# Layer with retention and windowed attention: conditioning sums gathered on VectorE, gate weights loaded later, a new order of the first microseconds, and the first block's mixed rows on VectorE

## The chip, the cores and the metric

The kernel runs on one core of a Trainium2 chip. The metric is device time in microseconds (us) of one execution. The engines are TensorE (PE, with its weight loads shown apart as PEld), VectorE (DVE), ScalarE (ACT), GpSimd (POOL) and SyncE (SP, which here only issues transfers). Each executes its own queue of instructions in order and waits there for data and buffers of the others.

## The reference, cut to what matters

One layer works on 2048 latent tokens of 1024 features and 256 context tokens. It is modulated by a conditioning vector `c`, or `c_ctx` for the context.

```python
shift, scale, gate = split(silu(c) @ w_ada + b_ada, 3)         # 1024 each
shift_c, scale_c, gate_c = split(silu(c_ctx) @ w_ada + b_ada, 3)
h  = rms_norm(x)   * (1 + scale)   + shift                     # 2048 x 1024
hc = rms_norm(ctx) * (1 + scale_c) + shift_c                   # 256 x 1024
rq, rk, rv, rg, aq, ak, av, ag = project(h, w_in)              # 1024 -> 3328 columns
_, crk, crv, _, _, cak, cav, _ = project(hc, w_in)
rq, rk, aq, ak = axial_rope(rq), axial_rope(rk), axial_rope(aq), axial_rope(ak)
s_fwd, s_bwd = retention_final_state(crk, crv, ...)            # starting states
ret_x = retention_branch(rq, rk, rv, rg, s_fwd, s_bwd)         # both directions, group norm, SiLU gate
att_x = windowed_gqa(aq, ak, av, cak, cav, sink) * silu(ag)    # window of 128 beside all context keys
x = x + gate * (concat(ret_x, att_x) @ w_out)
return rms_norm(x) * final_norm_w
```

## The kernel before, in words

Every matrix product is in three passes of TensorE: each fp32 operand is held as a rounded high part and a low part (the operand minus its high part), and the passes are high by high, high by low and low by high (`PASSES`). So each projection weight costs a rounding and a subtraction of 128x512 pieces, four of each for one weight of 1024x256. `load_w` does that: `hi` says who rounds, `lo` who subtracts, and with `lo="mix"` GpSimd takes the second piece of each of the two loads. `split` does the same to a projected, rotated tile (`hi_aq`, `lo_aq`).

The 2048 tokens are four groups of 512 (3, 2, 1, 0; group 3 first). The kernel has these stages.

**Start.** The tokens of group 3 come in transposed (`h2x`, eight feature slices `k` of 128x512), and so do the small parameters (`pr`) and the row of `c` (`row`). The sum of squares over features (`ss_x`) is made by four matmuls with ones on the pairwise sums of squares, and the diagonal blocks are taken out by VectorE (`own_x`). `roots` turns it into 1/rms (a power on GpSimd, `r_x`) and four diagonal tiles (`dg_x`), and `spread` puts the roots on all partitions (`rr_x`). Matmuls on ones (`warm`) fill TensorE's time meanwhile. `silu_row` spreads the row over the partitions (`pc`, then SiLU into `row`). For each `k`, `ada` loads two 128x1024 pieces of `w_ada` (`wss`) and `weigh` makes of each, with the row, one column of 128 sums: shift and scale of that slice (`mod`). `modulate` then makes the high and low parts of `h` (`h3h`, `h3l`), and TensorE puts them through the first three weights (`rg0`, `rq0`, `rq1`, the tiles `frg`, `frq`), whose pieces come in as `wr_s` and are split on the way.

**Projections of groups 3 and 2, with the context beside them.** TensorE goes through the weights `aq1`, `rq0`, `rq1`, then the context's `crk` and `crv` and the groups' `rk` and `rv`, for each of two pairs of heads. Beside that runs a list `spare` of small jobs, of which `background()` takes one after each unit: the context's norm, then eight jobs `column(k)`, each with two `weigh` of 128x1024 by `c_ctx` (`wss`, `room` holds the row), the modulation of one slice and its split into `hc`, and then nine jobs of `gate_columns`: the row of `c` once more and eight `weigh` for the gate (`wgt`, sums in `gcol`). In this stage every second `weigh` is done by GpSimd as a product, with the sum taken by a pass of ScalarE.

**Projections of groups 1 and 0**, and then **sixteen blocks of 128 tokens**: scores `S` of window and context keys, softmax, transposes, values, retention, and the output projection `pz`. The attention scores of the first blocks are woven into the last gate projection by the strings of `WEAVE`: one character pair per unit, `04s` standing for pieces of work put at step k=0. For the first block (b=0) of retention `first` holds keys, queries and states, and `ret_out` makes the gated retention rows `gr` and splits them into `mr` (high and low), from which `pz` starts.

## Time and profile before

| what | value |
|---|---|
| median of the three runs shown | 1163.0 us (1161.56 to 1398.94) |
| the profiled execution: time | 1162.4 us |
| the profiled execution: span in the trace | 1160.6 us |
| PE, DVE, ACT, POOL busy | 97%, 68%, 40%, 34% of the span |
| mean granted TensorE clock | 0.99 of full speed |

All stretches and starts below are us from the start of the span. The profiled execution has 1.8 us outside its span, and lies 0.6 us under the median.

### The profile page before, as it was taken

The page shows a single profiled execution, that of the slowest core. Times are in us where ns is not written, and L with a number is a line of the kernel's source. Part 1 is how long each engine was busy: PE and PEld are TensorE (multiplying, and loading weights), DVE is VectorE, ACT ScalarE, POOL GpSimd, SP SyncE. Part 2 cuts the span into 40 slices and gives each one's busy share as a digit, 9 for nine tenths or more (in the row PEclk, how much of TensorE's full clock was granted, in tenths as well). Part 3 has the DMA queues.
Part 4 walks back from the last instruction along what each step waited for, and adds up shares of the span by engine and source line. Part 5 has one row for each costly group of instructions (what it writes and reads, how often), then busy time and mean ns, then how long its engine had stood idle before and what let it go on. Part 6 is the DMA issues. An engine that isn't in the chain of part 4 may idle for free.

```text
span 1160.6 us, 18086 instructions
## 1 busy us (share of the span) xinstructions
PE 1130.3 (97%) x6290; PEld 974.3 (84%) x6290; DVE 792.4 (68%) x1884; ACT 467.8 (40%) x1026; POOL 399.9 (34%) x517
## 2 busy tenths in 40 slices
...
GB/s 318 322 153 264 234 232 310 168 146 87 158 198 180 182 93 99 151 104 150 88 118 276 69 177 249 106 135 133 136 131 133 133 132 132 132 132 132 96 56 36
DMA packets 139537, 182.24 MB, mean 157 GB/s; under 512 B 11315, under 2 KB 103091, under 8 KB 139318
## 3 DMA queue, kind: packets, MB, share of 16 engines
...
q14 instruction: 42, 0.34, 0.1%
...
## 4 chain that ended last, share of the span: by engine, by line
PE 80%; DVE 9%; DMA 4%; POOL 2%; ACT 2%; issue 2%; SPq 0%; POOLq 0%; DVEq 0%; ACTq 0%
PE pz L1209 14%; PE rv L354 8%; PE rk L341 8%; PE ag L341 6%; PE o L1172 6%; PE pt L1159 5%; PE aq L341 5%; PE rg L341 4%; PE rq L341 4%; PE S L743 3%; PE S L747 2%; PE u L470 2%; PE ak L341 2%; DVE wss L215 2%; PE av L341 1%
## 5 line engine op out<-in xcount | busy, mean ns | idle before, releaser
L765 POOL TENSOR_SCALAR p<-p,m 128x640 f32<-128x640 f32 (+1 forms) x128 | 102.2, 799 | 83.6 <-DVE m L764 82.4
L756 ACT ACTIVATE p<-p,m 128x641 f32<-128x641 f32 (+1 forms) x128 | 104.6, 817 | 62.5 <-DVE m L753 62.1
L1161 ACT ACTIVATE phl<-pt 128x512 fp32r<-128x512 f32 x156 | 92.6, 595 | 79.3 <-PE pt L1159 76.3
L1162 DVE TENSOR_TENSOR phl<-pt,phl 128x512 fp32r<-128x512 f32 x156 | 106.2, 682 | 24.1 <-ACT phl L1161 23.5
L749 DVE CUSTOM_DVE_ANT_0 p<-S,msk 128x640 f32<-128x640 f32 (+1 forms) x128 | 102.4, 800 | 13.1 <-PE S L747 6.9
L1209 PE MATMUL pz<-wg1h,ma 128*128 128x512 f32 x256 | 106.1, 419 | 0.1
L1209 PE MATMUL pz<-wg0h,mr 128*128 128x512 f32 x256 | 103.9, 409 | 1.3 <-POOL mr L109 0.8
L1159 PE MATMUL pt<-ident,p 128*128 128x128 f32 x624 | 93.2, 272 | 0.0
L1159 PEld LDWEIGHTS pt<-ident,p 128*128 128x128 f32 x624 | 75.3, 140 | 8.4
L743 PE MATMUL S<-kwin,aq 128*128 128x384 f32 (+1 forms) x256 | 79.4, 332 | 0.1
L446 ACT ACTIVATE vw<-v,wdec 128x128 fp32r<-128x128 f32 x128 | 43.6, 394 | 80.1 <-DVE v L459 80.1
L747 PE MATMUL S<-kctx,aq 128*128 128x256 f32 x256 | 71.1, 280 | 0.0
L1172 PE MATMUL o<-phl,vwin 128*128 128x512 f32 x184 | 62.2, 416 | 1.3 <-DVE phl L1162 0.8
L1209 PEld LDWEIGHTS pz<-wg0h,mr 128*128 128x128 f32 x256 | 48.1, 188 | 10.3 <-POOL mr L109 1.1
L1209 PEld LDWEIGHTS pz<-wg1h,ma 128*128 128x128 f32 x256 | 48.1, 188 | 7.9 <-POOL ma L1187 0.5
L743 PEld LDWEIGHTS S<-kwin,aq 128*128 128x128 f32 x256 | 48.0, 188 | 7.0 <-DVE m L749 1.6
L747 PEld LDWEIGHTS S<-kctx,aq 128*128 128x128 f32 x256 | 48.2, 188 | 5.2
L1209 PE MATMUL pz<-wg0l,mr 128*128 128x512 f32 x128 | 50.5, 394 | 0.0
L1209 PE MATMUL pz<-wg1l,ma 128*128 128x512 f32 x128 | 50.3, 393 | 0.0
L448 DVE SCALAR_TENSOR_TENSOR vw<-v,wdec,vw 128x128 fp32r<-128x128 f32 x128 | 39.8, 356 | 6.2 <-ACT vw L446 6.2
L1183 DVE TENSOR_TENSOR mf<-o,ob 64x256 f32<-64x256 f32 x64 | 26.7, 417 | 24.6 <-ACT ob L1180 23.9
L1172 PE MATMUL o<-phl,vctx 128*128 128x512 f32 x128 | 41.4, 403 | 0.2 <-DVE phl L1162 0.2
...
## 6 DMA issues: line engine op xcount, KB each, us to landing
wss<-in_wss SPq DMA_DIRECT2D x32, 512.0 KB, 7.0
...
xb<-in_xn SPq DMA_DIRECT2D x16, 512.0 KB, 4.0
...
st<-d_st SPq DMA_DIRECT2D x15, 512.0 KB, 3.3
...
x<-in_xt SPq DMA_DIRECT2D x12, 512.0 KB, 5.8
```

Source lines behind the costliest of these rows:

```text
L341: pe.matmul(ps, w[:, a, k, c0 : c0 + P], ht[b][:, k, :], start=(k == 0 and i == 0), stop=(k == NK - 1 and i == 2),)
L354: pe.matmul(ps, ht[a][:, k, t * P : (t + 1) * P], w[:, b, k, :], start=(k == 0 and i == 0), stop=(k == NK - 1 and i == 2),)
L743: i = pe.matmul(psc[:, o:512].rearrange("p (s t) -> p s t", t=P), AQ[b][:, h, :], C2["kwin"][:, kv, hl, ksel], start=(hl == 0), stop=(hl = ...
L747: pe.matmul(psc[:, 512:768], AQ[b][:, h, :], C2["kctx"][:, kv, hl], start=(hl == 0), stop=(hl == 1))
L749: dve.tensor_tensor_reduce(out=pb[:, j, 0:n], in0=psc[:, o : o + n], in1=mk, op0=ALU.add, op1=ALU.max, scale=1.0, scalar=-3e38, accum_out= ...
L756: act.activation(pb[:, j, 0 : n + 1], pb[:, j, 0 : n + 1], AF.Exp, bias=m4[:, 1, j : j + 1], scale=0.125, accum_out=m4[:, 2, j : j + 1],)
L765: PE["norm"] = pool.tensor_scalar(pb[:, j, 0:n], pb[:, j, 0:n], m4[:, 2, j : j + 1], 0.0, op0=ALU.mult, op1=ALU.add)
L1159: pe.transpose(ppt[:, j], pb[:, j, kt * P : (kt + 1) * P], ident)
L1161: PE["phl"] = act.activation(phl[:, 0], ppt, AF.Copy)
L1162: PE["low"] = dve.tensor_tensor(phl[:, 1], ppt, phl[:, 0], op=ALU.subtract)
L1172: pe.matmul(PO[kv], vt, PH[kt][:, hl], start=(kt == 0 and hl == 0), stop=(kt == nkt - 1 and hl == 1))
L1209: pe.matmul(PZ[n2], m[:, a, k % RH, :], WG[k // 4][c][:, k % 4, s], start=(k == 0 and i == 0), stop=(k == NK - 1 and i == 2),)
```

## The change

It has seven parts. (1) The loads of `pr` and of the row of `c` are issued by ScalarE, so SyncE's queue begins with the four loads of `h2x`. (2) The start's order is written out: twelve matmuls on ones, the two `pc`, then the sums of squares, of which ScalarE squares seven slices and VectorE one; twelve matmuls of one column each add them straight into 128x4 `ss_x`; `roots` uses ScalarE for the mean and the four `dg_x`; a tiny copy (`tick`) that reads the finished roots holds back VectorE's second `weigh`. (3) The low parts of the starting weights are all made by VectorE. (4) `weigh` is always one instruction of VectorE, and the nine jobs of the gate are appended to `spare` later, ahead of the second pair of heads, where `background` now takes two jobs. (5) `load_w` makes all low parts on VectorE, and `split` and the context's `hc` are rounded by ScalarE. (6) In `WEAVE` the second score piece of block 0 stands one step later. (7) For block 0 both parts of `mr` are made by VectorE.

```diff
...
-WEAVE = ("00 21 42 63", "04s 25 46y 67")
+WEAVE = ("00 21 42 63", "04 1s 25 46y 67")
...
-    nc.sync.dma_start(pr, par)
+    act.dma_start(pr, par)
...
-        def roots(self, on_dve=False):
-            r = rsm.tile([P, 2, 4], F32, tag="rs", name=f"r_{self.name}")
...
+        def roots(self):
+            r = self.r = rsm.tile([P, 2, 4], F32, tag="rs", name=f"r_{self.name}")
+            act.activation(r[:, 1, : self.nt], self.ss, AF.Identity, bias=eps1, scale=1.0 / D)
             pool.tensor_tensor(r[:, 0, : self.nt], r[:, 1, : self.nt], half4[:, : self.nt], op=ALU.pow)
...
-                if on_dve:
-                    PE["diag"] = dve.tensor_scalar(dst, ident, rt, None, op0=ALU.mult)
-                else:
-                    act.activation(dst, ident, AF.Copy, scale=rt)
+                PE["diag"] = act.activation(dst, ident, AF.Copy, scale=rt)
...
-    def weigh(w, row, a, idle=False):
-
-        if idle:
-            pool.tensor_tensor(w, w, row, op=ALU.mult)
-            act.activation(w, w, AF.Copy, accum_out=a)
-        else:
-            dve.scalar_tensor_tensor(w, w, 1.0, row, op0=ALU.mult, op1=ALU.mult, accum_out=a)
+    def weigh(w, row, a):
+
+        return dve.scalar_tensor_tensor(w, w, 1.0, row, op0=ALU.mult, op1=ALU.mult, accum_out=a)
...
-            rounded(hc[0][:, k, :], x)
+            rounded(hc[0][:, k, :], x, "act")
...
-                (pool if lo == "pool" or (lo == "mix" and j) else dve).tensor_tensor(w[:, 1, ks, :], r2, w[:, 0, ks, :], op=ALU.subtract)
+                dve.tensor_tensor(w[:, 1, ks, :], r2, w[:, 0, ks, :], op=ALU.subtract)
...
-        rounded(hi, src)
+        rounded(hi, src, "act")
...
+    act.dma_start(row0[0:1], crow[0:1])
+    x3 = half("h2x3", [P, NK, GT], F32)
+    for i in range(4):
+        nc.sync.dma_start(x3[:, 2 * i : 2 * i + 2], xt[3][:, 2 * i : 2 * i + 2])
...
+    warm(12)
+    for n in range(2):
+        pc0[n] = ptp.tile([P, GT], F32, tag="tp", name=f"pc0{n}")
+        fixed(pe.matmul(pc0[n], ones[0:1], row0[0:1, n * GT : (n + 1) * GT], start=True, stop=True))
...
-    for i in range(4):
-        sq = [tmp(f"sq_x3_{i}{j}") for j in range(2)]
-        act.activation(sq[0], x3[:, 2 * i], AF.Square)
-        dve.tensor_tensor(sq[1], x3[:, 2 * i + 1], x3[:, 2 * i + 1], op=ALU.mult)
-        dve.tensor_tensor(sq[0], sq[0], sq[1], op=ALU.add)
-        pe.matmul(pss, ones, sq[0], start=(i == 0), stop=(i == 3))
...
+            fixed(pe.matmul(s3.ss[:, t : t + 1], x[:, t * P : (t + 1) * P], ones[:, 0:1], start=False, stop=last and t == 3))
...
+    own_sums(sq[6], True)
+    warm(5)
+    s3.roots()
...
+            return dve.tensor_copy(tick, s3.r[:, 0, 0:1])
...
     ps3 = s3.spread()
-    warm(4)
+    warm(6)
...
-            (pool if n == "rg1" else dve).tensor_tensor(w[:, 1, ks, :], raws[n], w[:, 0, ks, :], op=ALU.subtract)
+            dve.tensor_tensor(w[:, 1, ks, :], raws[n], w[:, 0, ks, :], op=ALU.subtract)
...
-    spare += gate_columns()
...
-                W[x] = load_w(x[0], x[1] + x[0], lo="mix" if early else "dve", hi="act" if early else "pool")
+                W[x] = load_w(x[0], x[1] + x[0], hi="act" if early else "pool")
...
-                background()
+                background(2)
...
+    spare += gate_columns()
     retention(5, groups, ahead)
...
-        rounded(MR[b][:, 0], g)
-        pool.tensor_tensor(MR[b][:, 1], g, MR[b][:, 0], op=ALU.subtract)
+        rounded(MR[b][:, 0], g, "pool" if b else "dve")
+        (pool if b else dve).tensor_tensor(MR[b][:, 1], g, MR[b][:, 0], op=ALU.subtract)
```

What this does to the engines' queues is shown at three places. The first is TensorE's queue at the start, before: the two `pc`, then four wide sums of squares, then the first matmuls on ones.

```order
L205 MATMUL pc_127<-row_125,ones 128x512
L205 MATMUL pc_130<-row_125,ones 128x512
L933 MATMUL ss_x_138<-sq_x_00_139,ones 128x512
L933 MATMUL ss_x_138<-sq_x_10_145,ones 128x512
L933 MATMUL ss_x_138<-sq_x_20_151,ones 128x512
L933 MATMUL ss_x_138<-sq_x_30_157,ones 128x512
```

And the same place in the changed kernel, behind twelve matmuls on ones (of which the last is shown).

```order
L915 MATMUL warm_132<-wones 128x512
L921 MATMUL pc_145<-row_122,ones 128x512
L921 MATMUL pc_147<-row_122,ones 128x512
L930 MATMUL ss_x_151<-zero_149,ones 128x4
L935 MATMUL ss_x_151<-ones,sq_x_0_153 128x1 x4
L935 MATMUL ss_x_151<-ones,sq_x_4_157 128x1 x4
L935 MATMUL ss_x_151<-ones,sq_x_6_159 128x1 x4
```

The matmuls that wait for the last squares are now four of one column. The second place is VectorE's queue before, where the low parts of the weight `w_brq` for `rq1` are made (`m_aq` and `m_rq` are rotated projections, `lo_aq` a low part that needs `hi_aq`).

```order
L371 TENSOR_TENSOR m_aq_1187<-m_aq_1187,m_aq_1188 128x512
L329 TENSOR_TENSOR w_brq_1229<-wr_brq_0_1230,w_brq_1229 128x512
L378 TENSOR_TENSOR lo_aq_1196<-m_aq_1185,hi_aq_1195 128x512
L378 TENSOR_TENSOR lo_aq_1202<-m_aq_1187,hi_aq_1201 128x512
L329 TENSOR_TENSOR w_brq_1229<-wr_brq_1_1236,w_brq_1229 128x512
L366 TENSOR_TENSOR m_rq_1294<-rq_1242,rope_r_1292 128x512
```

GpSimd's queue at that place, before:

```order
L329 TENSOR_TENSOR w_brq_1229<-wr_brq_0_1230,w_brq_1229 128x512
L212 TENSOR_TENSOR wss_5_1_1311<-wss_5_1_1311,room 128x1024
L329 TENSOR_TENSOR w_brq_1229<-wr_brq_1_1236,w_brq_1229 128x512
L109 TENSOR_SCALAR hi_aq_1195<-m_aq_1185 128x512
L109 TENSOR_SCALAR hi_aq_1201<-m_aq_1187 128x512
L212 TENSOR_TENSOR wss_6_1_1322<-wss_6_1_1322,room 128x1024
```

VectorE's queue at that place in the changed kernel:

```order
L368 TENSOR_TENSOR lo_aq_1212<-m_aq_1201,hi_aq_1211 128x512
L260 TENSOR_TENSOR hc<-room,hc 128x256
L368 TENSOR_TENSOR lo_aq_1218<-m_aq_1203,hi_aq_1217 128x512
L205 SCALAR_TENSOR_TENSOR wss_4_1_1236,acc_112<-wss_4_1_1236,room 128x1024
L319 TENSOR_TENSOR w_brq_1243<-wr_brq_0_1244,w_brq_1243 128x512
L216 TENSOR_TENSOR mod<-acc_112,nbada 128x2
L319 TENSOR_TENSOR w_brq_1243<-wr_brq_0_1244,w_brq_1243 128x512
L319 TENSOR_TENSOR w_brq_1243<-wr_brq_1_1250,w_brq_1243 128x512
```

All four low parts of `w_brq` and the weighings stand on VectorE, and GpSimd has none of these six rows left. The third place is TensorE's queue behind the last matmul of `rq1`, before (the `pc` are those of the gate's row).

```order
L341 MATMUL rq_1368<-h2h,w_brq_1229 128x512
L205 MATMUL pc_1419<-room,ones 128x512
L205 MATMUL pc_1422<-room,ones 128x512
L354 MATMUL crk_1439<-w_brk_1330,hc 128x256 x24
L354 MATMUL crk_1465<-w_brk_1330,hc 128x256 x24
L354 MATMUL crv_1494<-w_brv_1425,hc 128x256 x24
```

And in the changed kernel:

```order
L331 MATMUL rq_1380<-h2h,w_brq_1243 128x512
L344 MATMUL crk_1443<-w_brk_1342,hc 128x256 x21
L344 MATMUL crk_1469<-w_brk_1342,hc 128x256 x21
L344 MATMUL crv_1495<-w_brv_1429,hc 128x256
L344 MATMUL crv_1525<-w_brv_1429,hc 128x256
L331 MATMUL rk_1555<-h3h,w_brk_1342 128x512
```

The `pc` of the gate's row have left this place (they stand behind the second pair's `crk`), and the last three matmuls of each `crk`, which need the last slice of `hc`, stand behind a piece of `rk`.

## Rows read from the trace of the kernel before

**Rows 1.** The page's part 1 (busy time, share of the span and instructions of each engine) and part 4 (the chain that ended last, its shares by engine).

```profile
PE 1130.3 (97%) x6290; PEld 974.3 (84%) x6290; DVE 792.4 (68%) x1884; ACT 467.8 (40%) x1026; POOL 399.9 (34%) x517
...
PE 80%; DVE 9%; DMA 4%; POOL 2%; ACT 2%; issue 2%; SPq 0%; POOLq 0%; DVEq 0%; ACTq 0%
```

**Rows 2.** The table of stretches. Columns: stretch, its length, busy time (and instructions) of PE, PEld, DVE, ACT, POOL, the granted TensorE clock as a share of full speed, the busy share of the DMA engines, GB/s.

```profile
0.00:10.00 10.00, 6.80 (x8) 2.32 (x9) 5.22 (x15) 4.53 (x7) 0.69 (x6) 1.00 0.73 262
10.00:20.00 10.00, 7.18 (x24) 3.56 (x24) 7.53 (x22) 2.87 (x5) 3.21 (x2) 0.84 1.02 395
30.00:60.00 30.00, 30.00 (x133) 24.50 (x132) 27.86 (x46) 10.80 (x19) 3.93 (x3) 1.00 0.92 323
150.00:160.00 10.00, 3.84 (x16) 2.54 (x14) 5.28 (x6) 1.16 (x3) 7.54 (x5) 1.00 0.71 246
160.00:170.00 10.00, 8.84 (x27) 7.06 (x28) 9.17 (x17) 2.34 (x4) 4.25 (x7) 0.66 0.78 222
180.00:190.00 10.00, 7.62 (x51) 7.42 (x50) 8.21 (x9) 2.87 (x8) 4.48 (x2) 0.83 0.90 277
700.00:710.00 10.00, 7.86 (x37) 5.44 (x38) 5.47 (x14) 8.35 (x14) 3.45 (x5) 1.00 0.96 325
710.00:1130.00 420.00, 419.89 (x2569) 372.72 (x2568) 331.57 (x975) 248.69 (x509) 225.45 (x322) 1.00 0.42 127
```

**Rows 3.** Instructions in order of time from the start to the first projection matmul, and one VectorE row some microseconds later. Columns: start, duration (of all where xN stands), engine, line, operation, output<-inputs, shapes, count, and in brackets the engine's idle time before it with what ended it.

```profile
0.72 0.39 SPq L79 DMA_DIRECT2D pr<-in_par  x1
...
1.55 1.77 SPq L924 DMA_DIRECT2D h2x<-in_xt  x4
...
9.73 0.63 ACT L930 ACTIVATE sq_x<-h2x 128x512 f32<-128x512 f32 x1 [0.67 <-DMA h2x<-in_xt]
...
10.62 0.69 DVE L932 TENSOR_TENSOR sq_x<-sq_x,sq_x 128x512 f32<-128x512 f32 x1
...
12.33 1.89 PE L919 MATMUL warm<-wones 128*128 128x512 bf16 x8
...
13.83 1.94 POOL L184 TENSOR_TENSOR r_x<-r_x,half 128x4 f32<-128x4 f32 x1 [12.54 <-DVE r_x L181]
...
15.81 1.94 DVE L189 TENSOR_SCALAR dg_x<-ident,r_x 128x128 f32<-128x128 f32 x4 [0.92 <-POOL r_x L184]
...
20.47 0.72 ACT L232 ACTIVATE h3h<-h2x,mod 128x512 fp32r<-128x512 f32 x1 [4.54 <-DVE h2x L231]
...
21.24 1.22 PE L997 MATMUL frg<-h3h,wrg 128*128 128x512 f32 x2 [0.48 <-ACT h3h L232]
...
29.12 1.25 DVE L226 TENSOR_TENSOR mod<-acc,nbada 128x2 f32<-128x2 f32 x1
```

**Rows 4.** The same view where the context's sums and roots are made (`ss_xc`, `r_xc`, `dg_xc`).

```profile
101.66 0.60 PE L168 MATMUL ss_xc<-ones,sqc 128*128 128x1 f32 x4 [0.70 <-DVE sqc L165]
...
102.72 0.70 POOL L184 TENSOR_TENSOR r_xc<-r_xc,half 128x2 f32<-128x2 f32 x1 [10.21 <-ACT r_xc L183]
...
103.44 0.40 ACT L191 ACTIVATE dg_xc<-ident,r_xc 128x128 f32<-128x128 f32 x1 [0.21 <-POOL r_xc L184]
```

**Rows 5.** Who TensorE waited for up to 420 us: total, times, longest.

```profile
PE rq L341 <- DVE w_brq L329: 7.3, 2, 6.1
...
PE crv L354 <- DVE w_brv L329: 2.4, 1, 2.4
```

**Rows 6.** Instructions in order of time in the context's stretch.

```profile
150.06 0.68 DVE L370 TENSOR_TENSOR m_aq<-m_aq,m_aq 128x512 f32<-128x512 f32 x1
...
150.66 0.68 DVE L371 TENSOR_TENSOR m_aq<-m_aq,m_aq 128x512 f32<-128x512 f32 x1
...
152.42 2.40 POOL L212 TENSOR_TENSOR wss<-wss,room 128x1024 f32<-128x1024 f32 x1 [2.86 <-DMA wss<-in_wss]
...
156.67 3.84 DVE L378 TENSOR_TENSOR lo_aq<-m_aq,hi_aq 128x512 fp32r<-128x512 f32 x2 [4.72 <-POOL hi_aq L109]
...
161.16 1.22 PE L341 MATMUL rq<-h2h,w_brq 128*128 128x512 f32 x2 [6.15 <-DVE w_brq L329]
...
168.20 4.68 DVE L329 TENSOR_TENSOR w_brk<-wr_brk,w_brk 128x512 fp32r<-128x512 f32 x4
...
171.80 1.98 PE L205 MATMUL pc<-room,ones 1*128 1x512 f32 x4
...
189.89 0.40 PE L341 MATMUL rk<-h3h,w_brk 128*128 128x512 f32 x1
```

**Rows 7.** VectorE's groups of instructions from 113.1 to 189.9 us: busy us, mean ns of one, and idle time before them.

```profile
L215 DVE SCALAR_TENSOR_TENSOR wss<-wss,room 128x1024 f32<-128x1024 f32 x8 | 9.7, 1214 | 0.0
```

**Rows 8.** VectorE's instructions from 250 to 262 us, in order of time.

```profile
261.24 0.69 DVE L366 TENSOR_TENSOR m_rk<-rk,rope_r 128x512 f32<-128x512 f32 x1 [12.35 <-PE rk L341]
```

**Rows 9.** The page's part 6 (transfers by line: count, KB each, median us from issue to landing).

```profile
wss<-in_wss SPq DMA_DIRECT2D x32, 512.0 KB, 7.0
```

**Rows 10.** Instructions in order of time at the passage to the blocks.

```profile
687.03 1.16 PE L790 MATMUL s<-first 128*128 128x128 f32 x8 [1.73 <-DMA first<-d_qkv]
...
706.19 0.62 POOL L109 TENSOR_SCALAR mr<-gr 128x512 fp32r<-128x512 f32 x1 [2.23 <-DVE gr L1195]
...
706.86 0.50 PE L1209 MATMUL pz<-wg0h,mr 128*128 128x512 f32 x1 [0.81 <-POOL mr L109]
...
708.21 0.73 PE L1209 MATMUL pz<-wg0h,mr 128*128 128x512 f32 x2 [0.45 <-POOL mr L1198]
```

More of the change, by code (lines that the diff above doesn't have):

```diff
@@ L223, in ada @@
             nc.sync.dma_start(w, wss[kc][:, j, :])
-            with behind(after[j]):
-                weigh(w, row, acc2[:, kc, which, j : j + 1], which and j)
+            with behind(after[j](i) if callable(after[j]) else after[j]):
+                i = weigh(w, row, acc2[:, kc, which, j : j + 1])
         dve.tensor_tensor(mod[:, kc, which], acc2[:, kc, which], nbada[:, kc:16:8], op=ALU.add)
@@ L312, in fine_rows, with load_w @@
         return rows
[L314 removed]
+    def load_w(name, uid, parts=(0, 1), w=None, fine=None, hi="pool"):
         ci = CHUNKS.index(name)
@@ L612, in column @@
             nc.sync.dma_start(wg, wgt[k])
-            weigh(wg, row2, gcol[:, k : k + 1], k % 2)
+            weigh(wg, row2, gcol[:, k : k + 1])
             if k == NK - 1:
@@ L934, in tile_hymba @@
-    s3.ss = rsm.tile([P, 4], F32, tag="ss", name="s_x3")
-    own = tmp("own_x3")
-    for t in range(4):
-        ts = slice(t * P, (t + 1) * P)
-        dve.scalar_tensor_tensor(
-            own[:, ts], pss[:, ts], 1.0, ident, op0=ALU.mult, op1=ALU.mult, accum_out=s3.ss[:, t : t + 1]
-        )
-    warm(4)
-    s3.roots(True)
-    warm(4)
+    fixed = tc.keep_in_program_order
+    warm(12)
+    for n in range(2):
+        pc0[n] = ptp.tile([P, GT], F32, tag="tp", name=f"pc0{n}")
+        fixed(pe.matmul(pc0[n], ones[0:1], row0[0:1, n * GT : (n + 1) * GT], start=True, stop=True))
@@ new lines, in silu0, with own_sums @@
+    def silu0(n):
+        fixed(act.activation(row0[:, n * GT : (n + 1) * GT], pc0[n], AF.Silu))
+    s3 = Stats(GT, "x3")
+    zero4 = rsm.tile([P, 4], F32, tag="zero", name="zero4", bufs=1)
+    dve.memset(zero4, 0.0)
+    s3.ss = ptp.tile([P, 4], F32, tag="tp", name="ss_x3")
+    fixed(pe.matmul(s3.ss, ones, zero4, start=True, stop=False))
+    def own_sums(x, last=False):
+        for t in range(4):
+            fixed(pe.matmul(s3.ss[:, t : t + 1], x[:, t * P : (t + 1) * P], ones[:, 0:1], start=False, stop=last and t == 3))
@@ new lines, in add, with square @@
+    def add(x, y):
+        fixed(dve.tensor_tensor(x, x, y, op=ALU.add))
+    sq = [tmp(f"sq_x3_{k}") if k < 4 else ld.tile([P, GT], F32, tag="ld", name=f"sq_x3_{k}") for k in range(NK)]
+    def square(k):
+        if k == 7:
+            fixed(dve.tensor_tensor(sq[k], x3[:, k], x3[:, k], op=ALU.mult))
+        else:
+            fixed(act.activation(sq[k], x3[:, k], AF.Square))
+    for i in range(2):
+        square(2 * i)
+        square(2 * i + 1)
+        add(sq[2 * i], sq[2 * i + 1])
+    add(sq[0], sq[2])
```

51 lines of the change are left out of this document (30 added, 21 removed).

## The prediction

> **What bounds the kernel now.** I read the busy times and the chain of waits first: TensorE is busy 97% of the span and carries 80% of the chain, VectorE 9% [rows 1]. So the change can only give what TensorE loses: 30 us of idle time, matmuls at the lower clock, and matmuls that are no work. The table of stretches says where that is. From 710 to 1130 us TensorE idles 0.1 us of 420, and from 30 to 60 us not at all [rows 2]. The losses are in three places. At the start the first projection matmul begins at 21.24 us [rows 3]; what TensorE does before are spreads, sums and matmuls on ones. Between 150 and 190 us it idles 6.16, 1.16 and 2.38 us in three slices, and in two of them its clock is 0.66 and 0.83 of full speed, which is a mixture of the levels 1.2 and 2.4 GHz [rows 2]. At the passage to the blocks it idles 2.14 us in one slice [rows 2] and 1.73 us at the first block's `s` [rows 10]. Everything below is about these three.
>
> **The change, part by part: the start.** The chain here is: last square, sum, roots, diagonals, spread, first `h3h`, first matmul. Before, the last square starts at 9.73 us when its data lands, and the first matmul at 21.24 [rows 3]: 11.5 us. Now the loads of `h2x` are first in SyncE's queue, at 0.72 instead of 1.55 us [rows 3], so I put the last square at 8.9. Between the last square's start and the last addition's end lay 1.6 us (9.73 to 10.62, and 0.69) [rows 3]: 10.5. The four last sums of one column take 0.6 us as in the context's sums [rows 4], at the lower clock twice that: 11.1 to 11.7. The mean on ScalarE is under 0.4 us: 11.4 to 12.1. The power on GpSimd is 0.70 us for the context and was 1.94 us here beside other work [rows 3, 4]; I take 1.0, and keep both: 12.1 to 14.0. Four diagonals at 0.40 on ScalarE [rows 4] against 1.94 for the four on VectorE [rows 3]: 13.7 to 15.6. The second `weigh` of slice 0 starts at the tick and ends 1.2 us after the power [rows 7], so it is done before the diagonals are. The spread's last piece, about 0.4 us, and then a scaling of about 0.75 us (a VectorE pass of 0.69 [rows 3]) and `h3h` 0.72 [rows 3] give 15.6 to 17.5. The six matmuls on ones behind the spread cost 0.24 each (1.89 for eight [rows 3]), at half speed 0.48, so they end at 15.5 to 18.9. The first matmul comes between 15.6 and 18.9, a gain of 2.3 to 5.6, and I take 3.9.
>
> How much of it lasts? From 30 to 60 us TensorE is full and VectorE is busy 27.86 of 30 us [rows 2], so VectorE has to follow the earlier pace. It takes over one low part per pair of slices, 0.6 us, and loses the 1.1 us by which `mod` was stretched (1.25 for two columns [rows 3], beside GpSimd's low part). It can follow, but with little room at slice 1, which now has four low parts in front. I keep **3.5 us** of it, range 1.5 to 5.
>
> A rule speaks against the first step. The load of `pr` moves to ScalarE's queue, and `h2x` was limited by its data: the wait of 0.67 before the last square is for that transfer [rows 3]. The Trainium skill, "DMA: Bandwidth & Descriptors", section "Issuing engines are not separate DMA queues", says in my words that transfers issued by different engines run on the same 16 engines. By that only the issue time of 0.83 us is gained, and no overlap beyond it, and no run here yet shows it. The chain above takes just that 0.83; without it the gain would be 3.1.
>
> **The context's stretch.** What holds TensorE is the second half of `rq1`'s weight: it waits for VectorE's low part, 7.3 us in two waits, and 2.4 us for the low part of `w_brv` [rows 5]. VectorE isn't slow there, it waits itself: 4.72 us for GpSimd's `hi_aq`, which stands behind a weighing of 2.40 us that began late, after 2.86 us of waiting for its load, and then its low parts take 1.92 each instead of 0.6 (3.84 for two) [rows 6]. The change takes weighings, low parts and roundings off GpSimd there. VectorE gets them: is it in time? Counting the changed order from the first weighing (113.2 us in the time of before) to the last low part of `rq1`'s weight, VectorE does 10 weighings of 1.2 us [rows 7], 36 passes of 128x512 at 0.60 from start to start [rows 6] (12 low parts of weights, 18 of rotations, 6 `lo_aq`), and 13 half-size passes plus small ones of about 5 us: 12.0 + 21.6 + 5 = 38.6 us, so 151.8. TensorE wants the first low part at about 150 and the last a few us later; it had it at 161.16 [rows 6]. So the 7.3 us go nearly whole. Next come four weighings, eight rotation passes, four low parts of `w_brk` and little else, 12 us: 163.5, where TensorE, having lost nothing, arrives at 161. Then two weighings, six passes and four low parts of `w_brv`, 9 to 10 us: 173. TensorE has two times 21 matmuls of `crk` and a piece of `rk` to fill part of that. The new bound is VectorE's queue, late by 1 to 3 us.
>
> The sum by slices: idle time 6.16 + 1.16 + 2.38 = 9.7 us, and clock 0.34 of 8.84 plus 0.17 of 7.62 = 4.3 us [rows 2], together 14.0. The clock fell when TensorE had stood still for 6.15 us [rows 6], so it should not fall if that wait goes. From this I take off 1 to 3 us that VectorE's queue is late, and 0 to 2.5 us for a new fall of the clock at such a wait: **11 us**, range 4 to 14. The two `pc` for the gate (1.98 us [rows 6]) leave here and come back later behind the second pair's `crk`: nothing, or 1.1 us more if the stretch behind them is slower; I take 0.5 off.
>
> Eight gate weighings on VectorE, 8 x 1.2 = 9.7 us, land in its idle time of 12.35 us before `m_rk` at 261.24 [rows 8]; they wait for the SiLU of the row, some 3 us, which TensorE's two `pc` push back in the same way. They fit with about nothing left. If that cover were gone, all 9.7 us would be late for `m_rk`. The roundings that move to ScalarE are counted at nothing: it is busy 40% of the span [rows 1] and 1.16 and 2.34 us of 10 in two of the slices here [rows 2]; behind it they would delay `hi_aq` as GpSimd did, by at most one pass in front of each.
>
> **The passage.** The second piece of the scores moves one step behind, which puts three projection matmuls, by the ones of the same width 0.24 us each [rows 3], so 0.7 us, ahead of the wait of 1.73 us for `first` [rows 10]: gain 0.7, or 0 if the load starts later by the same. For `mr`, TensorE waits 0.81 and 0.45 us [rows 10]. VectorE's subtraction is a pass of 0.69 [rows 3]; its rounding to `mr` has no row, and lies between GpSimd's 0.62 [rows 10] and a VectorE pass of 0.69 [rows 3]; both wait their turn behind score work on VectorE. I take 0.4 for both, range -0.8 to 1.2. Together **1.1 us**, range -0.8 to 1.9. The Trainium skill, "VectorE: DVE Perf Modes", section "The perf-mode tier table", gives a single-source fp32 copy within SBUF twice the rate; by that the rounding would take about half a pass, an estimate of 0.35 us from that page, and the sum would be 0.3 us better. No run here shows it so far.
>
> **Sum**: 3.5 + 11 - 0.5 + 1.1 = 15.1 us. From the profiled execution's 1162.4 us that gives 1147.3 us, and with the median 0.6 above it, **1147.9 us**.
>
> **The rivals.**
> *VectorE becomes the bound of the context's stretch.* VectorE's four low parts of `w_brk` take 4.68 us instead of 2.4 beside GpSimd [rows 6], and GpSimd still rounds `w_brk` and `w_brv`, eight times 0.62 [rows 10]. If each holds VectorE for its whole length, its queue is 5 us later, TensorE waits that long for `w_brv`, and the clock falls again, 2 us: the stretch gives 11 - 7 = 4, and the time is 1155. Against it: the eight weighings of the stretch also read two tensors beside a busy GpSimd, and took 1.21 us on the mean [rows 7]. The Trainium skill, "SBUF — State Buffer", section "SBUF: two separate sides", has that as a rule: a VectorE instruction with two SBUF inputs and a GpSimd instruction that reads SBUF exclude each other for a whole instruction; the row of 4.68 agrees.
> *Nothing is lost again.* VectorE's queue keeps up, the start gives 5, the stretch 14, the passage 1.9: 20.4, so 1142.6. Nothing in the rows forbids it, but VectorE must be on time at three weights in a row.
> *The start doesn't give.* If the first microseconds stay at the lower clock, the ones behind the spread end at 18.9 and slice 1 is late: 1 us instead of 3.5, 1150.4.
> *Slower than before: the gate's loads come one by one.* The eight weighings stand in one row of VectorE's queue ahead of `m_rk`. Each load takes 7.0 us [rows 9]. If five of them (those that find no buffer free) are issued only after the weighing before, each costs 7.0 + 1.2 us: 41 us, less the 12.35 us of cover [rows 8], 28.7 us late at `m_rk`; TensorE stands, and 28.7 - 15.1 over the median makes it 1176.6. It ends on the slower side from four such loads on (32.8 - 12.35 = 20.5, over 15.1). Against it: four of the five take the buffers of `w_brk` and `w_brv` rows, which VectorE has read before the first weighing; only the last needs the buffer of a weighing.
>
> **How the numbers follow.** The forecast with its own range, 1144 to 1152, gets 0.55; VectorE as the bound 0.22; nothing lost 0.12; no gain at the start 0.07; the slower case 0.04. The range that leaves out no more than 2 in 10 goes from 1142 to 1156.5. Faster by over 2% means under 1139.7, a gain of 23.3 us, beyond all the sums above: 0.05 for what they don't hold. Slower by over 2%, over 1186, needs all five loads and more: 0.01. Within 2%, about what a measurement of this kernel can tell from no change: 0.94.
>
> **What would show it.** In the profile after: the first `frg` matmul at 15.6 to 18.9 us; no wait of over 1.5 us of `rq` for `w_brq`; `rk` after the context (189.89 [rows 6]) about 15 us earlier; VectorE without idle time between 115 and 170 us; the wait of `s` for `first` near 1 us. The prediction is wrong if `crk` or `crv` waits over 4 us for low parts, if `m_rk` or what follows it makes TensorE wait near 260, or if TensorE's clock is below full in the stretch from 150 to 180.

## The result, and the profile after

The changed kernel takes 1148.6 us (median of four runs, 1148.17 to 1151.04), the kernel before 1162.3. The ratio is 0.9891 with a 95% interval of 0.987 to 0.9913; one execution of the kernel before, at 1398.9 us, was in a slower state and is left out of it. Run once more beside other kernels it took 1148.4, with a ratio of 0.9868 (0.9848 to 0.9889). The forecast was 1147.9. The profiled execution below took 1151.0 us (span 1149.2), 2.4 more than its median; a second profile, `a_again`, took 1147.35 (span 1145.6).

The table of stretches of the kernel after answers to [rows 2]. Columns: stretch, its length, busy time (and instructions) of PE, PEld, DVE, ACT, POOL, granted clock, DMA share, GB/s.

```profile
10.00:20.00 10.00, 9.90 (x40) 7.14 (x40) 5.04 (x10) 3.40 (x10) 1.04 (x1) 0.59 1.02 383
150.00:160.00 10.00, 9.91 (x45) 7.96 (x43) 10.00 (x18) 1.02 (x2) 5.34 (x4) 1.00 1.01 326
160.00:170.00 10.00, 7.49 (x53) 6.80 (x54) 10.00 (x19) 1.31 (x3) 2.42 (x5) 1.00 0.70 230
170.00:180.00 10.00, 10.00 (x70) 9.28 (x69) 1.82 (x4) 3.67 (x12) 0.00 (x0) 1.00 0.79 266
...
225.00:245.00 20.00, 20.00 (x138) 18.41 (x137) 15.04 (x32) 8.85 (x24) 2.84 (x4) 0.91 0.56 180
705.00:1120.00 415.00, 414.95 (x2530) 368.04 (x2529) 328.51 (x967) 246.90 (x506) 219.91 (x315) 1.00 0.41 125
```

From 150 to 160 us TensorE is busy 9.91 of 10, where it was 3.84, and its clock is full up to 180; VectorE has no idle time from 150 to 170 us. The clock of 0.59 at 10 to 20 us and of 0.91 at 225 to 245 is looked at below. Who TensorE waited for (total, times, longest), the answer to [rows 5] and to the waits of [rows 10]:

```profile
PE crv L344 <- DVE w_brv L319: 1.8, 1, 1.8
...
PE s L780 <- DMA first<-d_qkv: 1.3, 1, 1.3
...
PE crk L344 <- DVE w_brk L319: 0.8, 1, 0.8
```

The 7.3 us for `w_brq` are gone. What is left is 2.6 us for the low parts of `w_brk` and `w_brv`.

Where the time went is best read from the starts of the same TensorE instructions in each trace, us from the span's start. `frg` is the first projection matmul, `ss_xc` the context's sums, `cu` the first matmul behind the first pair's context, `cu` 2 the same of the second pair, `rq` 2 the first projection of groups 1 and 0, `s` the first block's retention.

| trace | `frg` | `ss_xc` | `cu` | `cu` 2 | `rq` 2 | `s` | span |
|---|---|---|---|---|---|---|---|
| before | 21.24 | 101.66 | 200.80 | 266.48 | 384.34 | 687.03 | 1160.6 |
| after | 19.62 | 100.22 | 185.39 | 254.63 | 373.17 | 676.09 | 1149.2 |
| `a_again` | 18.80 | 99.89 | 184.59 | 252.32 | 370.98 | 672.47 | 1145.6 |
| `s_old` | 21.65 | 102.34 | 187.70 | 256.94 | 375.54 | 677.86 | 1151.0 |
| `c_all_pool` | 18.69 | 99.23 | 197.27 | 266.50 | 384.37 | 688.32 | 1161.3 |
| `p_old` | 19.78 | 100.91 | 185.84 | 255.07 | 373.76 | 676.70 | 1151.9 |
| `c_weigh_pool` | 18.66 | 99.31 | 194.66 | 263.88 | 382.64 | 684.99 | 1158.1 |
| `c_hi_pool` | 19.89 | 101.34 | 191.37 | 259.18 | 377.03 | 678.67 | 1151.8 |
| `c_lo_mix` | 19.52 | 100.18 | 191.23 | 258.97 | 377.62 | 679.23 | 1152.4 |
| `c_gate_early` | 18.63 | 99.22 | 186.22 | 252.92 | 371.48 | 675.55 | 1150.2 |
| `n_brk_act` | 18.67 | 99.45 | 182.89 | 252.18 | 370.82 | 672.27 | 1145.4 |
| `n_sum4` | 20.38 | 100.81 | 185.85 | 253.58 | 372.32 | 674.58 | 1147.8 |
| `n_rows` | 18.82 | 100.02 | 186.04 | 254.64 | 373.35 | 675.46 | 1148.6 |
| `n_best` | 18.87 | 99.81 | 183.29 | 251.11 | 369.76 | 671.31 | 1144.7 |

Before to after: the start gives 1.4 us (1.8 in `a_again`), the context's stretch 14.0 more (14.4), the stretch of the gate's two `pc` takes 3.6 back (2.1), 0.7 (0.8) goes between there and `rq` 2, and from there to the end 0.2 (1.6) comes. The two `pc` (1.98 us) have moved from the context's stretch into the next, so 1.98 of the 14.0 and of the 3.6 are their move and nothing else.

### The profile page after: what moved, and what is told of

The parts are those of the page before. It is cut to its first block, busy times and chain, and to the rows that moved or that the text cites. A ratio compares the mean times of both kernels' runs of the same rounds, so it can differ in the third digit from the quotient of the medians.

```text
span 1149.2 us, 18100 instructions
## 1 busy us (share of the span) xinstructions
PE 1129.1 (98%) x6319; PEld 976.0 (85%) x6319; DVE 786.7 (68%) x1907; ACT 475.8 (41%) x1044; POOL 328.3 (29%) x459
## 4 chain that ended last, share of the span: by engine, by line
PE 81%; DVE 7%; issue 5%; DMA 4%; ACT 2%; POOL 1%; SPq 0%; POOLq 0%; DVEq 0%; ACTq 0%
PE pz L1243 14%; PE rv L344 8%; PE rk L331 7%; PE o L1206 6%; PE ag L331 6%; PE pt L1193 5%; PE aq L331 5%; PE rg L331 4%; PE rq L331 4%; PE S L733 3%; PE S L737 2%; PE u L460 2%; PE ak L331 2%; PE av L331 1%; DVE wss L205 1%
```

## The experiments

Each is an edit of the changed kernel; times are medians of its runs, and rows are of its profile.

**The kernel again, and three parts undone.** The first run has no edit.

> The changed kernel once more, as the measure for the runs beside it. If the 13.7 us gained are the kernel's own, it comes out at 1148.6 us within 1.5. The first profile of it was 2.4 us over its median; of that, 1.6 us is a stretch at a lower TensorE clock behind the gate's pc at 236 us. Theory: that fall of the clock comes and goes between executions, so this profile may lack it and then has a span near 1146.5. Rival: it belongs to the two pc, is in every execution, and the span is 1148 to 1149 again.

Measured 1148.4 us (1147.35 to 1150.23). The stretch behind the gate's `pc` in this profile:

```profile
225.00:245.00 20.00, 20.00 (x141) 18.01 (x141) 15.52 (x34) 8.16 (x22) 2.84 (x4) 1.00 0.60 198
```

The clock is 1.00 where it was 0.91. So the fall comes and goes between executions; it was 0.91 also in the profiles of `s_old`, `p_old` and `n_brk_act`, and 1.00 in those of `n_best` and `n_sum4`. It explains 1.5 us of the 2.4 by which the first profile lay high.

```diff
-    act.dma_start(pr, par)
+    nc.sync.dma_start(pr, par)
...
-    own_sums(sq[6], True)
-    warm(5)
-    s3.roots()
+    warm(4)
+    s3.roots(True)
```

> The changed kernel with its first microseconds as before (loads, sums of squares, roots, low parts of the starting weights). By the prediction the start is worth 3.5 us: 1152.1. By the trace after, where the first projection matmul comes only 1.6 us earlier and the later work 1.5 us earlier, it is worth 1.5: 1150.1. Rival: VectorE's pace between 20 and 60 us decides and the start is worth nothing: 1148.6. In the trace the first frg matmul should be back near 21.2 us and everything from 117 us on 1.5 us later.

Measured 1152.8 us (1151.99 to 1154.13), ratio 0.9905 (0.9885 to 0.9926): 4.4 over `a_again`, with intervals of the two ratios that just touch. The two profiles lie 5.4 us apart. The table says that 2.85 us of it are there at `frg` and 2.45 at `ss_xc`; 0.7 comes in the context, 1.5 with the fall of the clock at 236 us, and 0.8 at `s`. By these two traces the start itself is worth 2.5 us, but `frg` lies anywhere from 18.6 to 19.9 us in the ten profiles with the changed start, so one pair of traces fixes it only to about 1 us. VectorE's pace didn't swallow it.

```diff
+        if idle:
+            pool.tensor_tensor(w, w, row, op=ALU.mult)
+            return act.activation(w, w, AF.Copy, accum_out=a)
         return dve.scalar_tensor_tensor(w, w, 1.0, row, op0=ALU.mult, op1=ALU.mult, accum_out=a)
...
-            rounded(hc[0][:, k, :], x, "act")
+            rounded(hc[0][:, k, :], x)
...
-        rounded(hi, src, "act")
+        rounded(hi, src)
...
-                W[x] = load_w(x[0], x[1] + x[0], hi=...)
+                W[x] = load_w(x[0], x[1] + x[0], lo="mix" if early else "dve", hi=...)
```

> The changed kernel with GpSimd's share of the context's stretch given back: every second weighing there (with its sum on ScalarE), the second low parts of the early weights, and the roundings of split and of hc. The gate's row and loads stay late. By the theory (VectorE waits for GpSimd's hi_aq, which stands behind late weighings, and TensorE waits for VectorE's low part of w_brq) the 14 us between 117 and 190 us go again: 1160 to 1163. Rival: most of the gain came from moving the gate's pc and weighings out of this stretch; then it is under 1155.

Measured 1162.0 us (1159.87 to 1163.88), 13.6 over `a_again`; the stretch from `ss_xc` to `cu` is 98.0 us long, 84.7 in `a_again`, 99.1 before. TensorE's waits:

```profile
PE rq L334 <- DVE w_brq L322: 7.8, 2, 6.7
...
PE crk L347 <- POOL hc L109: 2.3, 1, 2.3
```

The first is that of before (7.3 us); the second is another of the same size, where TensorE waited 2.4 us for `w_brv` before. So the gain of the stretch is GpSimd's share: with it given back, the stretch is only 1.1 us shorter than before, though the two `pc` have left it.

```diff
-WEAVE = ("00 21 42 63", "04 1s 25 46y 67")
+WEAVE = ("00 21 42 63", "04s 25 46y 67")
...
-        rounded(MR[b][:, 0], g, "pool" if b else "dve")
-        (pool if b else dve).tensor_tensor(MR[b][:, 1], g, MR[b][:, 0], op=ALU.subtract)
+        rounded(MR[b][:, 0], g)
+        pool.tensor_tensor(MR[b][:, 1], g, MR[b][:, 0], op=ALU.subtract)
```

> The changed kernel with the passage to the blocks as before (the string of WEAVE, and mr of block 0 on GpSimd). By the prediction it is worth 1.1 us: 1149.7. By the trace after, where the end lies only 0.2 us better against the last projection than before, it is worth 0.2 to 0.4: 1149.0. Rival: VectorE's extra work at that place costs as much as it gives: 1148.6 or less.

Measured 1149.5 us (1148.24 to 1153.67), 1.1 over `a_again` with an interval too wide to call it (ratio 0.9881, 0.9859 to 0.9902). TensorE waits 2.0 us for `first` in its profile, which is the slowest of its five executions. In the changed kernel the wait is 1.3 in the first profile and less than 0.3 in `a_again`: it changes from one execution to the next.

**Which of GpSimd's three kinds of work held it?** Each alone was given back.

```diff
+        if idle:
+            pool.tensor_tensor(w, w, row, op=ALU.mult)
+            return act.activation(w, w, AF.Copy, accum_out=a)
```

> The changed kernel with only every second weighing of the context given back to GpSimd and ScalarE. Theory (the queue): with all three kinds of work on GpSimd the loss was 13.6 us because hi_aq and the low parts of w_brq stood behind weighings; with the weighings alone nothing that TensorE waits for stands behind them, except hc: 1148.4 to 1151. Rival (the weighings themselves): GpSimd's weighing of 2.4 us holds VectorE's passes over SBUF and waits for its load, and most of the 13.6 us comes back: 1157 or more.

Measured 1160.3 us (1158.05 to 1162.48), 12 over `a_again`: the rival was right, and the queue on GpSimd that I had made the cause is not needed. In order of time, where `rq1`'s weight is due:

```profile
148.41 4.88 POOL L206 TENSOR_TENSOR wss<-wss,room 128x1024 f32<-128x1024 f32 x2 [12.65 <-DVE w_brq L322]
...
150.84 1.06 ACT L207 ACTIVATE wss<-wss 128x1024 f32<-128x1024 f32 x1 [4.04 <-POOL wss L206]
...
151.90 1.13 ACT L111 ACTIVATE hi_aq<-m_aq 128x512 fp32r<-128x512 f32 x2
...
152.54 1.29 DVE L371 TENSOR_TENSOR lo_aq<-m_aq,hi_aq 128x512 fp32r<-128x512 f32 x1 [4.23 <-ACT hi_aq L111]
```

GpSimd's two weighings begin at 148.41. ScalarE's sum of the first stands in its queue ahead of `hi_aq`, which so comes at 151.90; VectorE's `lo_aq` waits 4.23 us for it and stands ahead of `w_brq`'s low parts, and TensorE waits 3.7 us, and 2.6 more for `hc`. It is the chain of before with ScalarE in GpSimd's place. The stretch from `ss_xc` to `cu` is 10.7 us longer than in `a_again`: TensorE's waits are 7.3 of it, 2.6 of them with the last slice of `hc`, and its clock is down to 0.69 from 150 to 160 us and to 0.66 from 170 to 180. By this trace the loss is made by a weighing whose product and sum are on two engines, with what VectorE needs behind one of them. One thing stands beside it untested: here and in `c_all_pool` the order of TensorE's queue came out as before, with all of `crk` ahead of `rk`, so the wait for `hc` has no piece of `rk` to cover it. What the order adds is not told apart.

```diff
-            rounded(hc[0][:, k, :], x, "act")
+            rounded(hc[0][:, k, :], x)
...
-        rounded(hi, src, "act")
+        rounded(hi, src)
```

> The changed kernel with only the roundings of split and of hc given back to GpSimd. Theory (the queue): GpSimd has little else there, hi_aq and hc come at once, and VectorE's lo_aq behind it isn't late: 1148.4 to 1150. Rival: each rounding on GpSimd holds VectorE (six of 0.6 us and eight of 0.4 in the stretch), VectorE's full queue is 5 us later, and TensorE waits at w_brk and w_brv: 1153.

Measured 1154.2 us (1153.34 to 1157.16), 5.8 over. TensorE's waits:

```profile
PE crk L344 <- DVE w_brk L319: 2.6, 1, 2.6
PE rq L331 <- DVE w_brq L319: 1.7, 1, 1.7
```

VectorE waits little for GpSimd (1.4 us in all), yet its six `lo_aq` take 0.98 us each on the mean, 0.70 in the kernel after. The stretch from `ss_xc` to `cu` is 90.0 us long, 84.7 in `a_again`: the rival's 5 us are there, through VectorE's queue.

```diff
-                W[x] = load_w(x[0], x[1] + x[0], hi=...)
+                W[x] = load_w(x[0], x[1] + x[0], lo="mix" if early else "dve", hi=...)
```

> The changed kernel with only the second low parts of the three early weights given back to GpSimd (1.27 us each, six of them). Theory (the queue): GpSimd is free and makes them in time, VectorE has 3.6 us less in its full queue: 1147 to 1149. Rival: GpSimd's two-input pass holds VectorE as long as it lasts, and nothing is saved: 1149 to 1151.

Measured 1154.0 us (1153.33 to 1155.18), 5.6 over, more than either theory had. Two rows beside each other, and TensorE's longest wait:

```profile
139.62 4.34 POOL L319 TENSOR_TENSOR w_brq<-wr_brq,w_brq 128x512 fp32r<-128x512 f32 x2 [15.99 <-ACT w_brq L111]
...
140.50 2.30 DVE L205 SCALAR_TENSOR_TENSOR wss<-wss,room 128x1024 f32<-128x1024 f32 x1
...
PE crk L344 <- ACT hc L111: 4.4, 1, 4.4
```

A weighing of VectorE takes 2.30 us instead of 1.2 beside GpSimd's subtractions. The 4.4 us are another thing: with this cost of VectorE the order of TensorE's queue came out with all of `crk`'s last matmuls ahead of the piece of `rk` that covers them in the kernel after. How much of the 5.6 is the holding and how much the order is not told apart.

The three alone cost 12.0, 5.8 and 5.6, together 13.6, so they don't add. That all three draw on the same slack of VectorE's queue fits this, but is argued and not shown.

**The gate's place.**

```diff
     spare += prep_ctx()
+    spare += gate_columns()
...
-                background(2)
+                background()
...
-    spare += gate_columns()
     retention(5, groups, ahead)
```

> The changed kernel with the nine jobs of the gate back in the list behind the context's, so that the row's two pc stand in the first pair's stretch again and the eight weighings (all on VectorE) behind it. Theory: VectorE's queue is the bound until 171 us, but the weighings come behind w_brv's low parts, ahead of m_rk, where VectorE idles 8 us: the two pc cost 2 us at either place, 1147.5 to 1150. Rival: VectorE is late for m_rk and for the vw of the first rows, and the move was worth 3 us or more: 1151.5 or more.

Measured 1151.6 us (1150.73 to 1152.97), 3.2 over. The rival's size, but not by its mechanism: TensorE's only wait for `vw` is 0.5 us. `cu` is 1.6 us later (the `pc` stand ahead of it again), at `cu` 2 it is 0.6 and at `rq` 2 0.5. The other 2.6 come at `s`, which waits 2.4 us for its load, a wait that changed by about 1 us between two executions of the changed kernel; whether the place of the gate matters there stays open.

**Beyond the change: what holds it now?**

```diff
-                W[x] = load_w(..., hi="act" if early else "pool")
+                W[x] = load_w(..., hi="act" if x in order[:5] else "pool")
```

> The changed kernel with the high parts of the first pair's w_brk and w_brv rounded by ScalarE instead of GpSimd. Theory (a GpSimd rounding holds VectorE's passes over two SBUF tensors): in the profile after, four passes of VectorE beside those roundings took 0.3 to 0.4 us too long, 1.5 us in all, and TensorE waits 0.8 us for w_brk and 1.8 us for w_brv; without them these waits shrink by 1.5 to 2.5: 1146 to 1147. Rival: on ScalarE the roundings stand behind the context's modulations, which wait for VectorE, and come later: 1148.4 or more.

Measured 1147.4 us (1147.18 to 1148.05), 1.0 under `a_again`, with ratios of 0.9866 and 0.9868 that don't tell them apart. The profile does tell the mechanism. First the kernel after: VectorE, GpSimd and TensorE around `w_brk`.

```profile
149.08 0.69 DVE L319 TENSOR_TENSOR w_brq<-wr_brq,w_brq 128x512 fp32r<-128x512 f32 x1
...
155.56 1.63 DVE L205 SCALAR_TENSOR_TENSOR wss<-wss,room 128x1024 f32<-128x1024 f32 x1
...
157.12 0.56 DVE L216 TENSOR_TENSOR mod<-acc,nbada 128x2 f32<-128x2 f32 x1
...
158.79 0.76 DVE L260 TENSOR_TENSOR hc<-room,hc 128x256 fp32r<-128x256 f32 x1
...
154.66 5.37 POOL L109 TENSOR_SCALAR w_brk<-wr_brk 128x512 fp32r<-128x512 f32 x4 [52.77 <-DVE m_rq L361]
...
176.07 0.40 PE L331 MATMUL rk<-h3l,w_brk 128*128 128x512 f32 x1
```

GpSimd's four roundings take 5.37 us, 0.62 each elsewhere [rows 10], and beside them VectorE's weighing takes 1.63, `mod` 0.56 and `hc` 0.76. With the roundings on ScalarE:

```profile
153.73 2.38 ACT L111 ACTIVATE w_brk<-wr_brk 128x512 fp32r<-128x512 f32 x4 [5.74 <-DMA wr_brk<-in_win]
...
154.85 1.21 DVE L205 SCALAR_TENSOR_TENSOR wss<-wss,room 128x1024 f32<-128x1024 f32 x1
...
156.00 0.15 DVE L216 TENSOR_TENSOR mod<-acc,nbada 128x2 f32<-128x2 f32 x1
...
157.27 0.42 DVE L260 TENSOR_TENSOR hc<-room,hc 128x256 fp32r<-128x256 f32 x1
...
160.45 5.20 PE L344 MATMUL crk<-w_brk,hc 128*128 128x256 f32 x42
```

The same VectorE work takes 1.21, 0.15 and 0.42, all of `crk`'s first 42 matmuls run without a wait, and `cu` comes 1.7 us earlier than in `a_again`, of which 0.4 is there at `ss_xc` already. In this profile 1.5 of it went with the clock at 236 us. That both engines stretch is what the Trainium skill, "SBUF — State Buffer", section "SBUF: two separate sides", says of a VectorE instruction with two SBUF inputs beside a GpSimd instruction that reads SBUF; the trace agrees, with 0.34 to 0.42 us lost by each of the three.

```diff
-    own_sums(sq[0])
...
     add(sq[4], sq[5])
-    own_sums(sq[4])
+    add(sq[0], sq[4])
...
     add(sq[6], sq[7])
+    add(sq[0], sq[6])
     silu0(1)
-    own_sums(sq[6], True)
+    own_sums(sq[0], True)
```

> The changed kernel with all squares added up by VectorE first and four one-column sums in place of twelve. In the profile after, the twelve took 5.3 us (24 passes at 0.22, at the lower clock) and ended at 14.05 us, where the prediction had 11.1 to 11.7. Theory (the sums hold the roots): with one addition of 0.7 more and eight passes of 0.22 they end near 13.1, the first projection matmul comes 1 us earlier, and the time is 1147.4. Rival: VectorE's pace from slice 1 on decides, TensorE waits for h3h instead, and the time stays at 1148.4.

Measured 1149.4 us (1149.11 to 1150.96), 1.0 longer. The rows of VectorE and TensorE at its start:

```profile
11.56 1.22 DVE L205 SCALAR_TENSOR_TENSOR wss<-wss,row 128x1024 f32<-128x1024 f32 x1
...
12.71 0.69 DVE L938 TENSOR_TENSOR sq_x<-sq_x,sq_x 128x512 f32<-128x512 f32 x1
...
13.45 1.86 PE L935 MATMUL ss_x<-ones,sq_x 128*128 128x1 f32 x8 [5.47 <-DVE sq_x L938]
...
20.38 0.73 PE L1031 MATMUL frg<-h3h,wrg 128*128 128x512 f32 x2 [0.30 <-ACT h3h L222]
```

The first weighing (11.56) came between the last two additions, so the sums began at 13.45 and `frg` at 20.38. The edit didn't do what it was meant to. With later sums `frg` is 0.8 us later than in the first profile after, and outside the 18.6 to 19.9 of the other executions; the 1.0 us of the time is not told apart from `a_again` by the ratios (0.9884 and 0.9868).

```diff
-        nc.sync.dma_start(t[0:1], crow[i : i + 1])
+        nc.sync.dma_start(t, crow[i * P : (i + 1) * P])
...
-            pe.matmul(ps, ones[0:1], t[0:1, s], start=True, stop=True)
-            act.activation(t[:, s], ps, AF.Silu)
+            act.activation(t[:, s], t[:, s], AF.Silu)
```

> The changed kernel with the rows of c_ctx and of the gate loaded already spread over the partitions (512 KB each), so that the four pc matmuls of the two rows are gone. Theory (the pc and the lower clock behind them are lost time): each pair costs 1.98 us of TensorE, and behind the first the clock is at the lower level for 3 to 4 us, behind the second in some executions: 4 to 7 us less, 1141.5 to 1144.5. Rival: the half megabyte in front of the loads of wss makes the context's weighings late, VectorE's queue slips, and TensorE waits at w_brq and w_brk: 1147 or more.

Measured 1150.3 us (1149.39 to 1151.04), 2 longer by the medians, which the ratios (0.989 and 0.9868) don't tell apart, though TensorE has 4 us less to do. Its waits:

```profile
PE rq L329 <- DVE w_brq L317: 2.3, 1, 2.3
PE aq L329 <- DVE w_baq L317: 1.7, 1, 1.7
```

TensorE is ahead by the `pc`'s 2 us at 102 us and then waits 4.0 for VectorE's low parts of `w_baq` and `w_brq`. VectorE's queue is what the stretch lasts, so the `pc` were nearly free there. The larger loads have a part in it: VectorE's first weighing begins at 112.49 us, 111.01 in `a_again`, as VectorE waits 2 us longer for a small load, and its last low part of `w_brq` is 2.6 us later. How much of the 4.0 that makes isn't told apart.

```diff
     add(sq[4], sq[5])
-    own_sums(sq[4])
...
-    own_sums(sq[6], True)
+    last_add = add(sq[4], sq[6])
+    own_sums(sq[4], True)
...
-        ada(st0, "ada", row0, k, 0, (PE["scaled"],) * 2 if k else (None, ticked))
+        ada(st0, "ada", row0, k, 0, (PE["scaled"],) * 2 if k else (last_add, ticked))
```

The edit above stands beside that of `n_brk_act`.

> The kernel with the first pair's roundings on ScalarE, and at the start eight one-column sums (slices 0 to 3 as they are ready, 4 to 7 added up first) with VectorE's first weighing held behind the last addition. In the run with four sums that weighing had slipped between two additions, the first frg matmul came 0.8 us later than in the changed kernel (20.38 against 19.62) and the time was 1.0 us longer. Theory (the last one-column sum sets the start, and the start passes to the end one for one): the sums end near 13.2 instead of 14.05, the first frg matmul comes 0.8 us earlier, near 18.8, and the time is 1146.6 against 1147.4 of the kernel with the roundings alone. Rival: with the sums out of the way the next thing is late (the weighing for slice 0, a weight piece's load), the first matmul stays near 19.6 and the time at 1147.4.

Measured 1146.7 us (1146.47 to 1148.03), ratio 0.9868 (0.9846 to 0.9889), the lowest median here, 1.7 under `a_again`; the ratios don't tell the two apart. The last sums and the first matmul:

```profile
11.42 1.86 PE L935 MATMUL ss_x<-ones,sq_x 128*128 128x1 f32 x8 [1.02 <-DVE sq_x L938]
...
18.87 0.73 PE L1033 MATMUL frg<-h3h,wrg 128*128 128x512 f32 x2
```

`frg` is at 18.87 as expected, but it was at 18.80 in `a_again` and at 18.67 in `n_brk_act`, with twelve sums. So the spread of that moment between executions, 18.6 to 19.9 us, is as large as the edit, and the theory of the last sum isn't shown by this run. The roots begin at 13.32 us, where they began at 13.37 in `a_again`: the eight sums ended no earlier than those twelve.

## Why the prediction was right, and where its terms were off

**The bound.** That the loss was in three places, and that the rest would stay as it is, held: from 705 to 1120 us TensorE idles 0.05 us. Of the signs, the wait for `w_brq` is gone, the clock is full from 150 to 180, VectorE idles 0.03 of the 55 us from 115 on, and `s` waits 1.3 us. `rk` after the context comes 13.8 us earlier (176.07), where I had about 15, and `frg` at 19.62 missed its 15.6 to 18.9; at 18.80 in `a_again` it is just inside.

**The start**: 3.5 forecast, 1.4 to 2.5 in the traces; the times of `s_old` say 4.4, within about 3 by the intervals, so that the term was too large is a reading of traces alone. What failed in its chain is the step of the four last sums. I had them at 0.6 to 1.3 us behind the last addition, from the context's row [rows 4]. But that row of four is two sums, two passes each: four sums are eight passes, 1.86 us in `n_best` and `n_sum4`, and here earlier sums still stand in the queue ahead of them. The start of the kernel after, in order of time, and last the twelve sums of `a_again`:

```profile
8.77 5.28 PE L935 MATMUL ss_x<-ones,sq_x 128*128 128x1 f32 x24 [0.69 <-DVE sq_x L938]
9.07 0.62 ACT L946 ACTIVATE sq_x<-h2x 128x512 f32<-128x512 f32 x1
...
10.02 0.69 DVE L938 TENSOR_TENSOR sq_x<-sq_x,sq_x 128x512 f32<-128x512 f32 x1
...
14.08 0.26 ACT L180 ACTIVATE r_x<-ss_x,eps 128x4 f32<-128x4 f32 x1 [3.90 <-PE ss_x L935]
...
14.43 1.04 POOL L181 TENSOR_TENSOR r_x<-r_x,half 128x4 f32<-128x4 f32 x1 [13.13 <-ACT r_x L180]
...
15.49 1.28 ACT L185 ACTIVATE dg_x<-ident,r_x 128x128 f32<-128x128 f32 x4 [1.15 <-POOL r_x L181]
...
18.85 0.72 ACT L222 ACTIVATE h3h<-h2x,mod 128x512 fp32r<-128x512 f32 x1 [1.55 <-DVE h2x L221]
...
19.62 0.73 PE L1031 MATMUL frg<-h3h,wrg 128*128 128x512 f32 x2
...
9.03 4.30 PE L935 MATMUL ss_x<-ones,sq_x 128*128 128x1 f32 x24
```

Twelve sums are 24 passes and took 5.28 us, 0.22 each, at a granted clock that was 0.61 from 7.5 to 10 us and 0.50 from there to 15; the last additions are done at 10.7, but the queue of sums holds the roots until 14.08 where I had the mean at 11.1 to 11.7. In `a_again` the clock was still 1.00 from 7.5 to 10 us, and the sums took 4.30. So this moment goes with the clock: in the ten profiles with this start the roots begin at 13.1 to 14.4 us, and `frg` follows 5.2 to 5.8 us behind them. The power (1.04) and the diagonals (1.28 for four) came as put, or better. The loads gave 0.66 us of the 0.83, as the last square starts at 9.07 against 9.73 [rows 3]; it is 9.33 in `a_again`.

**The context**: 11 forecast, 14.0 and 14.4 measured. The forecast let the gate's two `pc` leave here and come back later at the same price; without their 1.98 us it is 12.0 and 12.5, inside its range. The count of VectorE's queue was right: last low part of `w_brq` at 149.7 (I had 151.8, less the start's gain), no idle time, TensorE late by 2.6 us at `w_brk` and `w_brv`, 0.9 in `a_again` (forecast 1 to 3). What was too dear is the clock: I took off up to 2.5 us for a new fall, and it didn't fall from 110 to 180 us. The rival of VectorE as the bound was there in its mechanism, at some 1.3 us instead of 7 (the stretch is 83.4 us long in `n_brk_act`, 84.7 in `a_again`); `c_hi_pool` shows the price where more roundings stay on GpSimd.

**The gate**: 0.5 forecast. `cu` to `cu` 2 lasts 3.6 us longer (2.1), and 1.6 (0.1) without the two `pc`. The rows:

```profile
234.45 1.98 PE L199 MATMUL pc<-room,ones 1*128 1x512 f32 x4
236.36 7.52 PE L344 MATMUL crv<-w_brv,hc 128*128 128x256 f32 x48
...
245.40 1.22 DVE L205 SCALAR_TENSOR_TENSOR wgt<-wgt,room 128x1024 f32<-128x1024 f32 x1
...
249.39 0.69 DVE L356 TENSOR_TENSOR m_rk<-rk,rope_r 128x512 f32<-128x512 f32 x1 [2.55 <-PE rk L331]
```

The weighings did end ahead of `m_rk`, with 2.55 us to spare. The two `pc` came back at 1.98 us as counted. The 1.5 us between the two profiles are the clock behind them (`crv` 7.52 us, 6.02 in `a_again`), which I had at 0 or 1.1: it falls in some executions and not in others.

**The roundings on ScalarE** were counted at nothing. From `cu` 2 to `rq` 2 the kernel loses 0.7 to 0.8 us, for which the forecast has no term. One wait of TensorE there, in `a_again` and in `c_hi_pool`:

```profile
PE pvx L530 <- DVE x L221: 1.0, 1, 1.0
...
PE pvx L530 <- DVE x L221: 0.2, 1, 0.2
```

In the three profiles in which GpSimd rounds for `split` (before, `c_all_pool`, `c_hi_pool`) this wait is 0.2 us and the stretch 117.9 long; in the eleven in which ScalarE does, it is 0.9 to 1.2 us, and the stretch 118.5 to 118.8. How the rounding delays `x` is not shown.

**The passage**: 1.1 forecast; 0.2 and 1.6 from `rq` 2 to the end by the two profiles, and 1.1 by the times of `p_old`, which its interval doesn't tell from nothing. The rows of `mr`:

```profile
694.50 0.42 DVE L113 CAST mr<-gr 128x512 fp32r<-128x512 f32 x1
...
694.98 0.50 PE L1243 MATMUL pz<-wg0h,mr 128*128 128x512 f32 x1 [0.56 <-DVE mr L113]
...
695.58 0.69 DVE L1232 TENSOR_TENSOR mr<-gr,mr 128x512 fp32r<-128x512 f32 x1
```

The rounding took 0.42 us, the subtraction 0.69 on the same engine. The Trainium skill, "VectorE: DVE Perf Modes", section "The perf-mode tier table", was nearer with its doubled rate than my bounds of 0.62 to 0.69.

So by the traces the sum came out in part by luck: a start that was too large, and the loss at the roundings that it didn't have, met a context that was 1 to 1.5 us too small. The mechanism of the context, 11 of the 15.1 us, is the one that the runs show.
